# A decoder trunk in split fp32: the weights' products read their moving columns as two halves in turn

## The chip, the core and the metric

The kernel runs on one core of a Trainium2 chip. It is one program, launched once. The time is that of the device in microseconds (us); three runs of the kernel before took 2107.32 to 2107.49 us, with a median of 2107.39 us. The core's engines are TensorE (PE, with its weight loads shown apart as PEld), VectorE (DVE), ScalarE (ACT), GpSimd (POOL) and the queue engine SyncE (SP), each with its own stream of instructions; they wait for one another by semaphores. Tiles lie in SBUF, 128 partitions wide; TensorE writes into accumulators in PSUM.

## What is computed

The reference is two layers of a decoder on 256 tokens of width 2048, in float32. Cut to what matters:

```python
def reference(x, ...):                       # x: (1, 256, 2048)
    for i in range(2):
        h = rms_norm(x, attn_norm[i])
        if i == 0:   # 16 heads of 128: q, k, v = h @ wq, h @ wk, h @ wv; norm and rotary per head
            y = moba_attention(h, ...)       # causal within the one block of 256 keys, then @ wo
        else:        # low rank: (h @ wq_a) -> norm -> @ wq_b;  (h @ wkv_a) -> norm -> @ wkv_b
            y = mla_attention(h, ...)        # 16 heads of 128 plus 64 rotary dims, then @ wo
        x = x + y
        h = rms_norm(x, ffn_norm[i])
        g = conv3(h @ w_gate) + conv_b       # causal, per channel, over tokens; D_FF = 5632
        x = x + (silu(g) * (h @ w_up)) @ w_down
    return x
```

With 256 tokens nearly all arithmetic is tokens times weights. Every weight is read once (387.01 MB are read from HBM in all).

## The kernel before

**Three products for one.** Weights and tokens are float32. Each operand is split into a high part (rounded to float32r) and a low part (the rest). A product of tokens and weights is then the sum of three float32r products: high × high, high × low and low × high. The low × low product is left out. Attention's own small products use plain float32 for the first 128 tokens and the three parts for the others.

**The stream of weights.** The host lays all weights out in the order of their use, in 370 units. A unit is one DMA of up to 1 MB (128 partitions × 2048 numbers) into one of three `raw` buffers, issued on SP (`Stream.load`, L66). It holds four pieces of 128 × 512 (or 288). `Stream.split` (L92) makes the parts of each piece: ACT copies it into `whi` (L104) and DVE takes the difference into `wlo` (L105). There are five buffers of each part, each with room for 64 more numbers, so that a part can begin at a chosen address (`starts`, L156).

**By token** (`tok_major`, L227). For q, k, v and the low-rank projections the tokens are the stationary operand (128 tokens) and the weights move, 512 columns at a time. One piece is one slice of 128 of the contraction: 2 halves of the tokens × 3 parts = 6 products of 512 columns (L235), into one accumulator of 128 × 512 for each half of the tokens.

**By feature** (`feat_major`, L251). For the output projections, gate, up, down and `wq_a` the weights are stationary (128 × 128) and the 256 tokens move. A piece is four slices of the contraction: 4 × 3 = 12 products of 256 columns (L261, L262, L263), into an accumulator of 128 × 256. The moving operands are tiles of tokens' parts: `h` (the normed input, 16 slices), `a` (the gated activation, 44 slices), `oT` (attention's output, 16 slices), and `cqT` and `ckvT` (stationary operands by token). In each, a slice holds 256 numbers of the high part and then 256 of the low part, that is 2 KB:

```python
self.h = t[:, H_START : H_START + KD * 2 * S].rearrange("p (k s) -> p k s", k=KD)   # L277, S = 256
nc.scalar.activation(self.h[:, j, :S], xT[:, j, :], AF.Copy, scale=g)               # L279, high
lo, xT[:, j, :], g, hi.bitcast(F32), op0=ALU.mult, op1=ALU.subtract                 # L285, low
mm(o, w_hi, src[:, kt, :S], start=first and k == 0, ...)                            # L261, its read
```

**Who reads the accumulators.** Four accumulators rotate (`ps_acc`). By token, `Heads.evac` (L361, ACT), `evac_parts` (L604, ACT and DVE), `evac_values` (L615, ACT) and `kva_evac` (L836, ACT) copy them out. By feature, `residual` (L344, DVE) adds one to the residual stream `xT`; `FTile.evac_gate` (L739) and `FTile.product` (L764), both on DVE, read gate's and up's; `cq_part` (L914) reads those of `wq_a`.

**The order.** The program is a list of quanta, one for each piece of weights, in the order of the stream. Around each quantum stand the other engines' tasks: `at(q, f)` issues a task right after quantum q, `first(q, f)` right before it. The loop at the end (L1060) issues for each quantum the splits of the pieces ahead (up to four), the products of the piece, and then its tasks. Nothing is reordered later, so each engine's stream is this order.

**The stages**, with the times that the trace gives: MoBA's q, k, v and heads from 5 us, its output projection from 303, gate and up of layer 0 from 395, its down projection from 874 to about 1114, the low-rank projections and MLA's heads after that, their output projection from 1310, gate and up of layer 1 from 1386, and its down projection from 1862 to the end at 2101.

Of the kernel before, what the change touches and what calls it, by code (L numbers as in the profile page):

```python
# [52 lines left out]

class Stream:
# [37 lines left out]
    def split(self, upto):  # L92
        while self.split_to < min(upto, len(self.pieces)):
# [6 lines left out]
            lo = self.part_pool.tile([P, 512 + ROOM], F32R, name="wlo")[:, c : c + 512]  # L100
            if i == 0:
                self.nc.vector.tensor_copy(hi[:, :n], w)
            else:
                self.nc.scalar.copy(hi[:, :n], w)  # L104
            self.nc.vector.tensor_tensor(  # L105
                lo[:, :n], w, hi[:, :n].bitcast(F32), op=ALU.subtract
            )
# [8 lines left out]
def trunk(ctx: ExitStack, tc: tile.TileContext, a, out):  # L116
# [110 lines left out]
    def tok_major(state, lhs, kt, k_last, t_hi, t_lo, n):  # L227
# [5 lines left out]
        def product(t, part):  # L233
            c = (S if part == 2 else 0) + t * P
            mm(  # L235
                state["acc"][t][:, :n], src[:, kt, c : c + P], (t_lo if part == 1 else t_hi)[:, :n],
                start=kt == 0 and part == 0, stop=kt == k_last and part == 2,
            )
# [12 lines left out]
    def feat_major(state, rhs, k0, k_last, first, t_hi, t_lo, n, half=0):  # L251
# [6 lines left out]
        for k in range(n // P):  # L258
            kt = k0 + k
            w_hi, w_lo = t_hi[:, k * P : (k + 1) * P], t_lo[:, k * P : (k + 1) * P]  # L260
            mm(o, w_hi, src[:, kt, :S], start=first and k == 0, stop=False, skip_group_check=True)  # L261
            mm(o, w_hi, src[:, kt, S:], start=False, stop=False, skip_group_check=True)  # L262
            mm(o, w_lo, src[:, kt, :S], start=False, stop=kt == k_last, skip_group_check=True)  # L263


    class Norm:
# [7 lines left out]
        def high(self, j):  # L274
            if self.h is None:
                t = keep.tile([P, KD * 2 * S + 64], F32R, name="h")
                self.h = t[:, H_START : H_START + KD * 2 * S].rearrange("p (k s) -> p k s", k=KD)  # L277
            g = par[:, self.gain_col + j : self.gain_col + j + 1]
            nc.scalar.activation(self.h[:, j, :S], xT[:, j, :], AF.Copy, scale=g)  # L279

        def low(self, j):
            g = par[:, self.gain_col + j : self.gain_col + j + 1]
            hi, lo = self.h[:, j, :S], self.h[:, j, S:]
            nc.vector.scalar_tensor_tensor(
                lo, xT[:, j, :], g, hi.bitcast(F32), op0=ALU.mult, op1=ALU.subtract  # L285
# [58 lines left out]
    def residual(state, j, half):  # L344
        nc.vector.tensor_tensor(
            xT[:, j, :], xT[:, j, :], state["acc"][:, half * S : (half + 1) * S], op=ALU.add
        )
# [5 lines left out]
    class Heads:  # L353
# [7 lines left out]
        def evac(self):  # L361
# [6 lines left out]
            for t in range(NT):  # L368
                dst = self.x[:, t].rearrange("p n d -> p (n d)")
                src = self.state["acc"][t][:, : n * dh]  # L370
# [98 lines left out]
    class Head:  # L469
# [79 lines left out]
        def parted(self):  # L549
            oT = self.oT()  # L550
            hi, lo = oT[:, self.h, :S], oT[:, self.h, S:]
            nc.scalar.copy(hi, self.o[:, :S])
            nc.vector.tensor_tensor(lo, self.o[:, :S], hi.bitcast(F32), op=ALU.subtract)
# [17 lines left out]
    def moba_tiles(g):  # L571
        if g == 0:
            env["oT"] = att_pool.tile([P, H, 2 * S], F32R, name="oT", bufs=1)
# [144 lines left out]
    def open_ffn(layer):  # L718
# [6 lines left out]
        ffn["a"] = ffn["pool"].tile([P, NF, 2 * S], F32R, name="a", bufs=1)  # L725
# [4 lines left out]
    class FTile:  # L730
# [8 lines left out]
        def evac_gate(self):  # L739
            self.g = ffn["g"][self.j % 2]  # L740
            nc.vector.tensor_tensor(  # L741
                self.g[:, 2:], self.gate["acc"][:, :S], self.norm.rstd_b, op=ALU.mult
# [21 lines left out]
        def product(self):  # L764
            nc.vector.tensor_tensor(self.c, self.c, self.up["acc"][:, :S], op=ALU.mult)
# [56 lines left out]
    def open_mla():  # L822
# [4 lines left out]
        env["ckvT"] = att_pool.tile([P, 4, 2 * S], F32R, name="ckvT", bufs=1)  # L827
        env["cqT"] = att_pool.tile([P, 4, 2 * S], F32R, name="cqT", bufs=1)
# [350 lines left out]
```

## Time and profile before

| | |
|---|---|
| median of three runs | 2107.39 us |
| span of the profiled execution | 2105.5 us |
| TensorE busy | 2089.8 us, 16,732 records of products |
| weight loads busy | 2013.4 us, beside the products |
| VectorE busy | 1418.3 us |
| ScalarE busy | 1137.8 us |
| moved by DMA | 391.83 MB, 186 GB/s in the mean |
| granted TensorE clock | 1.000 |

The profiled execution's own time is its span of 2105.5 us, from its first to its last instruction; the median of the runs is 1.9 us above it. Products are pipelined: a row of 256 columns is shown with 276 ns, but the next one starts before it ends. The pace of products is read from their starts, or from a stretch's length over the number of products in it. One float32 product of the attention heads stands in the trace as up to two records.

### The profile page before, as it was taken

What the parts mean: (1) busy time and instruction counts of PE and PEld (TensorE: products, weight loads), DVE (VectorE), ACT (ScalarE), POOL (GpSimd) and SP (SyncE); (2) the same over time, 40 slices, a digit from 0 to 9 for tenths busy, and PEclk for the clock granted to TensorE, in tenths of its full rate; (3) what the DMA queues carried; (4) which work ended last, traced back from release to release, by engine and by line L of the source; (5) the groups of instructions that cost most, each with busy time, mean ns of one, the idle gap of its engine ahead of it and who ended that gap; (6) DMA issues with size and microseconds to landing.
All of it is one profiled execution on the core that took longest, in us unless ns stands there. A gap on an engine that the chain in (4) does not pass through costs nothing.

```text
span 2105.5 us, 42253 instructions
## 1 busy us (share of the span) xinstructions
PE 2089.8 (99%) x16732; PEld 2013.4 (96%) x16732; DVE 1418.3 (67%) x3084; ACT 1137.8 (54%) x2242; POOL 45.3 (2%) x37
## 2 busy tenths in 40 slices
PE   9999999999999999999999999999999999999999
PEld 7788889999999999999999789999999999999999
DVE  6777776766666766655556886777666667665554
ACT  6555555655555555555455675655555555544443
POOL 0000000000000000000000110000000000000000
PEclk9999999999999999999999999999999999999999
DMA  7445445555555555555554433555555555555553
GB/s 271 160 160 180 160 167 194 189 193 200 190 192 200 191 191 200 198 189 195 201 188 151 172 122 120 184 195 186 198 198 187 197 200 187 195 206 204 196 207 131
DMA packets 59382, 391.83 MB, mean 186 GB/s; under 512 B 6960, under 2 KB 10032, under 8 KB 13232
## 3 DMA queue, kind: packets, MB, share of 16 engines
q1 hardware_dynamic: 59040, 388.87, 52.1%
q8 instruction: 131, 2.15, 0.4%
q14 instruction: 67, 0.55, 0.1%
q10 hardware_dynamic: 144, 0.26, 0.0%
HBM read 387.01 MB, written 2.10 MB: 185 GB/s over the span
## 4 chain that ended last, share of the span: by engine, by line
PE 92%; DVE 5%; ACT 1%; issue 1%; DMA 1%; POOL 1%; SPq 0%; ACTq 0%; POOLq 0%
PE acc L263 26%; PE acc L261 26%; PE acc L262 26%; PE acc L235 11%; DVE wlo L105 1%; DVE junk L379 1%; DVE qk L405 1%; PE tp L449 1%; POOL hr L392 1%; PE tp L520 0%; ACT whi L104 0%; DMA raw<-in_moba_wq 0%; ACT qk L374 0%; PE sc L545 0%; DMA xT<-in_xT 0%
## 5 line engine op out<-in xcount | busy, mean ns | idle before, releaser
L105 DVE TENSOR_TENSOR wlo<-raw,whi 128x512 fp32r<-128x512 f32 (+1 forms) x1480 | 1000.3, 684 | 402.1 <-ACT whi L104 399.2
L104 ACT CAST whi<-raw 128x512 fp32r<-128x512 f32 (+1 forms) x1479 | 871.9, 614 | 464.0 <-PE acc L262 212.5
L261 PE MATMUL acc<-h,whi 128*128 128x256 f32 x2880 | 795.3, 276 | 0.0
L263 PE MATMUL acc<-h,wlo 128*128 128x256 f32 x2880 | 794.9, 276 | 0.0
L262 PE MATMUL acc<-h,whi 128*128 128x256 f32 x2880 | 794.9, 276 | 0.0
L262 PEld LDWEIGHTS acc<-h,whi 128*128 128x128 f32 x2880 | 540.7, 188 | 0.0
L261 PEld LDWEIGHTS acc<-h,whi 128*128 128x128 f32 x2880 | 540.6, 188 | 0.0
L263 PEld LDWEIGHTS acc<-h,wlo 128*128 128x128 f32 x2880 | 540.6, 188 | 0.0
L261 PE MATMUL acc<-a,whi 128*128 128x256 f32 x1408 | 388.6, 276 | 0.0
L262 PE MATMUL acc<-a,whi 128*128 128x256 f32 x1408 | 388.6, 276 | 0.0
L263 PE MATMUL acc<-a,wlo 128*128 128x256 f32 x1408 | 388.6, 276 | 0.0
L235 PE MATMUL acc<-whi,h 128*128 128x512 f32 (+1 forms) x896 | 277.4, 382 | 0.5 <-ACT whi L104 0.5
L261 PEld LDWEIGHTS acc<-a,whi 128*128 128x128 f32 x1408 | 264.3, 188 | 0.0
L262 PEld LDWEIGHTS acc<-a,whi 128*128 128x128 f32 x1408 | 264.3, 188 | 0.0
L263 PEld LDWEIGHTS acc<-a,wlo 128*128 128x128 f32 x1408 | 264.3, 188 | 0.0
L235 PEld LDWEIGHTS acc<-whi,h 128*128 128x128 f32 x896 | 164.7, 188 | 30.9 <-ACT whi L104 1.4
L235 PE MATMUL acc<-wlo,h 128*128 128x512 f32 (+1 forms) x448 | 170.2, 380 | 2.8 <-DVE wlo L105 2.8
L261 PE MATMUL acc<-oT,whi 128*128 128x256 f32 x512 | 143.5, 280 | 0.0
L263 PE MATMUL acc<-oT,wlo 128*128 128x256 f32 x512 | 141.7, 277 | 0.0
L262 PE MATMUL acc<-oT,whi 128*128 128x256 f32 x512 | 141.6, 277 | 0.0
L741 DVE TENSOR_TENSOR g<-acc,rstd_b 128x256 f32<-128x256 f32 x88 | 37.5, 426 | 125.7 <-PE acc L263 122.8
L748 ACT ACTIVATE c<-g,par 128x256 f32<-128x256 f32 x88 | 53.1, 603 | 108.3 <-DVE g L741 108.3
(173 smaller groups left out, 1626.7 us busy)
## 6 DMA issues: line engine op xcount, KB each, us to landing
raw<-in_ffn_gu SPq DMA_DIRECT2D x176, 1024.0 KB, 4.8
raw<-in_ffn_down SPq DMA_DIRECT2D x88, 1024.0 KB, 4.8
raw<-in_moba_wk SPq DMA_DIRECT2D x16, 1024.0 KB, 4.9
raw<-in_moba_wv SPq DMA_DIRECT2D x16, 1024.0 KB, 4.8
raw<-in_moba_wo SPq DMA_DIRECT2D x16, 1024.0 KB, 4.8
raw<-in_mla_wo SPq DMA_DIRECT2D x16, 1024.0 KB, 4.8
raw<-in_moba_wq SPq DMA_DIRECT2D x13, 1024.0 KB, 4.8
raw<-in_mla_wkv_a SPq DMA_DIRECT2D x8, 576.0 KB, 3.8
```

Of the source, the lines that this page charges most:

```text
L104: self.nc.scalar.copy(hi[:, :n], w)
L105: self.nc.vector.tensor_tensor(lo[:, :n], w, hi[:, :n].bitcast(F32), op=ALU.subtract)
L235: mm(state["acc"][t][:, :n], src[:, kt, c : c + P], (t_lo if part == 1 else t_hi)[:, :n], start=kt == 0 and part == 0, stop=kt == k_last a ...
L261: mm(o, w_hi, src[:, kt, :S], start=first and k == 0, stop=False, skip_group_check=True)
L262: mm(o, w_hi, src[:, kt, S:], start=False, stop=False, skip_group_check=True)
L263: mm(o, w_lo, src[:, kt, :S], start=False, stop=kt == k_last, skip_group_check=True)
L379: nc.vector.tensor_tensor_reduce(out=junk[:, : self.dh], in0=self.x[:, t, i], in1=self.x[:, t, i], scale=1.0, scalar=0.0, op0=ALU.mult, op ...
L392: nc.gpsimd.tensor_tensor(self.r, ms, mhalf[:, : NT * n], op=ALU.pow)
L405: nc.vector.scalar_tensor_tensor(self.x[:, t, i], self.x[:, t, i], self.r[:, c : c + 1], g, op0=ALU.mult, op1=ALU.mult,)
L449: nc.tensor.transpose(tp[:, (i * NT + t) * P : (i * NT + t + 1) * P], flat[:, t, c : c + P], ident)
L741: nc.vector.tensor_tensor(self.g[:, 2:], self.gate["acc"][:, :S], self.norm.rstd_b, op=ALU.mult)
L748: nc.scalar.activation(self.c, self.g[:, 2:], AF.Identity, bias=par[:, cb : cb + 1], scale=self.cw(2))
```

## The change

Three helpers are new. `halves` cuts a run of numbers into its first and second half; `woven` reads such a pair of halves in turn (first of the one, first of the other, second of the one, and so on); `unwoven` undoes this for a run that holds the two in turn.

The tokens' parts (`h`, `a`, `oT`, `cqT`, `ckvT`) get a new layout. A slice of 2 KB held 256 tokens' high parts and then 256 tokens' low parts; now it holds, for the first 128 tokens, their high and their low parts, and then the same for the other 128. So the two halves of one part lie 1 KB apart. A product by feature reads its 256 columns in turn from these two halves. A product by token reads its 512 columns in turn from the first and the last 256 columns of the piece of weights, again 1 KB apart; the pieces of 288 are now held in two runs of 144, 1 KB apart.

The accumulators' columns come out in turned order, since TensorE writes them one after the other as before. All who read them (those named above) now step over every second number of PSUM and write, or meet, the two halves in the usual order. The stationary operands are the same runs of 128 numbers, though by token at other addresses. The attention heads' own products are not changed. The number of instructions of each kind is the same for products, copies and transfers, and their order on each engine too.

The diff, without those hunks that do the same for further tiles (`oT`, `a`, `cqT`, `ckvT`, `kva_evac`, `kva_turn`, `cq_part`):

```diff
--- before.py
+++ after.py
@@ -49,6 +49,18 @@
 BY_TOKEN, BY_FEATURE = (8, 8), (24, 56)
 
 H_START = 8
+
+
+def halves(o):
+    return o.rearrange("p (t s) -> p t s", t=2)
+
+
+def woven(o):
+    return o.rearrange("p t s -> p s t")
+
+
+def unwoven(o):
+    return o.rearrange("p (s t) -> p t s", t=2)
 
 
 class Stream:
@@ -98,13 +110,15 @@
             b, c = self.starts(u, j)
             hi = self.part_pool.tile([P, 512 + ROOM], F32R, name="whi")[:, b : b + 512]
             lo = self.part_pool.tile([P, 512 + ROOM], F32R, name="wlo")[:, c : c + 512]
+            o_hi, o_lo = hi, lo
+            if n < 512:
+                o_hi, o_lo = (halves(o)[:, :, : n // 2] for o in (hi, lo))
+                w = halves(w)
             if i == 0:
-                self.nc.vector.tensor_copy(hi[:, :n], w)
+                self.nc.vector.tensor_copy(o_hi, w)
             else:
-                self.nc.scalar.copy(hi[:, :n], w)
-            self.nc.vector.tensor_tensor(
-                lo[:, :n], w, hi[:, :n].bitcast(F32), op=ALU.subtract
-            )
+                self.nc.scalar.copy(o_hi, w)
+            self.nc.vector.tensor_tensor(o_lo, w, o_hi.bitcast(F32), op=ALU.subtract)
             self.parts[i] = (hi, lo, n)
             self.split_to += 1
 
@@ -231,9 +245,9 @@
         src = lhs()
 
         def product(t, part):
-            c = (S if part == 2 else 0) + t * P
+            w = halves(t_lo if part == 1 else t_hi)[:, :, : n // 2]
             mm(
-                state["acc"][t][:, :n], src[:, kt, c : c + P], (t_lo if part == 1 else t_hi)[:, :n],
+                state["acc"][t][:, :n], src[:, kt, t, int(part == 2)], woven(w),
                 start=kt == 0 and part == 0, stop=kt == k_last and part == 2,
             )
 
@@ -258,9 +272,10 @@
         for k in range(n // P):
             kt = k0 + k
             w_hi, w_lo = t_hi[:, k * P : (k + 1) * P], t_lo[:, k * P : (k + 1) * P]
-            mm(o, w_hi, src[:, kt, :S], start=first and k == 0, stop=False, skip_group_check=True)
-            mm(o, w_hi, src[:, kt, S:], start=False, stop=False, skip_group_check=True)
-            mm(o, w_lo, src[:, kt, :S], start=False, stop=kt == k_last, skip_group_check=True)
+            hi, lo = (woven(src[:, kt, :, part]) for part in range(2))
+            mm(o, w_hi, hi, start=first and k == 0, stop=False, skip_group_check=True)
+            mm(o, w_hi, lo, start=False, stop=False, skip_group_check=True)
+            mm(o, w_lo, hi, start=False, stop=kt == k_last, skip_group_check=True)
 
 
     class Norm:
@@ -274,15 +289,17 @@
         def high(self, j):
             if self.h is None:
                 t = keep.tile([P, KD * 2 * S + 64], F32R, name="h")
-                self.h = t[:, H_START : H_START + KD * 2 * S].rearrange("p (k s) -> p k s", k=KD)
+                self.h = t[:, H_START : H_START + KD * 2 * S].rearrange(
+                    "p (k t a s) -> p k t a s", k=KD, t=NT, a=2
+                )
             g = par[:, self.gain_col + j : self.gain_col + j + 1]
-            nc.scalar.activation(self.h[:, j, :S], xT[:, j, :], AF.Copy, scale=g)
+            nc.scalar.activation(self.h[:, j, :, 0], halves(xT[:, j, :]), AF.Copy, scale=g)
 
         def low(self, j):
             g = par[:, self.gain_col + j : self.gain_col + j + 1]
-            hi, lo = self.h[:, j, :S], self.h[:, j, S:]
+            hi, lo = self.h[:, j, :, 0], self.h[:, j, :, 1]
             nc.vector.scalar_tensor_tensor(
-                lo, xT[:, j, :], g, hi.bitcast(F32), op0=ALU.mult, op1=ALU.subtract
+                lo, halves(xT[:, j, :]), g, hi.bitcast(F32), op0=ALU.mult, op1=ALU.subtract
             )
 
         def scaled(self, j):
@@ -342,9 +359,8 @@
 
 
     def residual(state, j, half):
-        nc.vector.tensor_tensor(
-            xT[:, j, :], xT[:, j, :], state["acc"][:, half * S : (half + 1) * S], op=ALU.add
-        )
+        x, acc = halves(xT[:, j, :]), unwoven(state["acc"][:, half * S : (half + 1) * S])
+        nc.vector.tensor_tensor(x, x, acc, op=ALU.add)
 
     def store(j):
         nc.sync.dma_start(out[:, j, :], xT[:, j, :])
@@ -366,8 +382,8 @@
                 self.x = att_pool.tile([P, NT, n, dh], F32, name="qr", bufs=1)
             self.ss = small.tile([P, NT, n], F32, name="ss")
             for t in range(NT):
-                dst = self.x[:, t].rearrange("p n d -> p (n d)")
-                src = self.state["acc"][t][:, : n * dh]
+                dst = halves(self.x[:, t].rearrange("p n d -> p (n d)"))
+                src = unwoven(self.state["acc"][t][:, : n * dh])
                 if self.scale is None:
                     nc.scalar.copy(dst, src)
                 else:
...
@@ -603,18 +620,18 @@
 
     def evac_parts(state, key, scale):
         v0, v1 = env[key]
-        hi, lo = v0[:, 0], v0[:, 1]
-        first_, second = (state["acc"][t][:, :512] for t in range(NT))
+        hi, lo = halves(v0[:, 0]), halves(v0[:, 1])
+        first_, second = (unwoven(state["acc"][t][:, :512]) for t in range(NT))
         r = scale()
         nc.scalar.activation(hi, first_, AF.Copy, scale=r[:, 0:1])
         nc.vector.scalar_tensor_tensor(
             lo, first_, r[:, 0:1], hi.bitcast(F32), op0=ALU.mult, op1=ALU.subtract
         )
-        nc.scalar.activation(v1, second, AF.Copy, scale=r[:, 1:2])
+        nc.scalar.activation(halves(v1), second, AF.Copy, scale=r[:, 1:2])
 
     def evac_values(state, key, scale):
         for t in range(NT):
-            dst, src = env[key][:, t, :], state["acc"][t][:, :512]
+            dst, src = halves(env[key][:, t, :]), unwoven(state["acc"][t][:, :512])
             if scale is None:
                 nc.scalar.copy(dst, src)
             else:
...
@@ -739,7 +756,8 @@
         def evac_gate(self):
             self.g = ffn["g"][self.j % 2]
             nc.vector.tensor_tensor(
-                self.g[:, 2:], self.gate["acc"][:, :S], self.norm.rstd_b, op=ALU.mult
+                halves(self.g[:, 2:]), unwoven(self.gate["acc"][:, :S]), halves(self.norm.rstd_b),
+                op=ALU.mult,
             )
 
         def conv_last(self):
@@ -762,16 +780,15 @@
             nc.vector.tensor_tensor(self.c, self.c, self.norm.rstd_b, op=ALU.mult)
 
         def product(self):
-            nc.vector.tensor_tensor(self.c, self.c, self.up["acc"][:, :S], op=ALU.mult)
+            c = halves(self.c)
+            nc.vector.tensor_tensor(c, c, unwoven(self.up["acc"][:, :S]), op=ALU.mult)
 
         def high(self):
-            nc.scalar.copy(ffn["a"][:, self.j, :S], self.c)
+            nc.scalar.copy(ffn["a"][:, self.j, :, 0], halves(self.c))
 
         def low(self):
-            a_ = ffn["a"]
-            nc.vector.tensor_tensor(
-                a_[:, self.j, S:], self.c, a_[:, self.j, :S].bitcast(F32), op=ALU.subtract
-            )
+            hi, lo = ffn["a"][:, self.j, :, 0], ffn["a"][:, self.j, :, 1]
+            nc.vector.tensor_tensor(lo, halves(self.c), hi.bitcast(F32), op=ALU.subtract)
 
     def plan_gate_up(layer, norm):
         for j in range(NF):
...
```

More of the change, by code (lines that the diff above doesn't have):

```diff
@@ L550, in parted @@
             oT = self.oT()
-            hi, lo = oT[:, self.h, :S], oT[:, self.h, S:]
-            nc.scalar.copy(hi, self.o[:, :S])
-            nc.vector.tensor_tensor(lo, self.o[:, :S], hi.bitcast(F32), op=ALU.subtract)
+            hi, lo = oT[:, self.h, :, 0], oT[:, self.h, :, 1]
+            o = halves(self.o[:, :S])
+            nc.scalar.copy(hi, o)
+            nc.vector.tensor_tensor(lo, o, hi.bitcast(F32), op=ALU.subtract)
         def plan(self, q, q_values):
@@ L572, in moba_tiles @@
         if g == 0:
-            env["oT"] = att_pool.tile([P, H, 2 * S], F32R, name="oT", bufs=1)
+            env["oT"] = att_pool.tile([P, H, NT, 2, P], F32R, name="oT", bufs=1)
         env["qT", g] = (
@@ L724, in open_ffn @@
         ffn["pool"] = ffn["stack"].enter_context(tc.tile_pool(name=f"ffn{layer}", bufs=2))
-        ffn["a"] = ffn["pool"].tile([P, NF, 2 * S], F32R, name="a", bufs=1)
+        ffn["a"] = ffn["pool"].tile([P, NF, NT, 2, P], F32R, name="a", bufs=1)
         ffn["g"] = [ffn["pool"].tile([P, S + 2], F32, name=f"g{i}", bufs=1) for i in range(2)]
@@ L826, in open_mla @@
         env["ckv"] = att_pool.tile([P, NT, 2 * KVN], F32, name="ckv", bufs=1)
-        env["ckvT"] = att_pool.tile([P, 4, 2 * S], F32R, name="ckvT", bufs=1)
-        env["cqT"] = att_pool.tile([P, 4, 2 * S], F32R, name="cqT", bufs=1)
-        env["oT"] = att_pool.tile([P, H, 2 * S], F32R, name="oT", bufs=1)
+        env["ckvT"] = att_pool.tile([P, 4, NT, 2, P], F32R, name="ckvT", bufs=1)
+        env["cqT"] = att_pool.tile([P, 4, NT, 2, P], F32R, name="cqT", bufs=1)
+        env["oT"] = att_pool.tile([P, H, NT, 2, P], F32R, name="oT", bufs=1)
         env["qr0"] = att_pool.tile([P, 8, P], F32, name="qr0", bufs=1)
@@ L838, in kva_evac @@
             nc.scalar.activation(
-                env["ckv"][:, t, half * KVN : (half + 1) * KVN], state["acc"][t][:, :KVN],
+                halves(env["ckv"][:, t, half * KVN : (half + 1) * KVN]),
+                unwoven(state["acc"][t][:, :KVN]),
                 AF.Copy, scale=n3.rstd[:, t : t + 1],
@@ L888, in kva_turn @@
         g = par[:, C_GKVA + r : C_GKVA + r + 1]
-        hi, lo = env["ckvT"][:, r, :S], env["ckvT"][:, r, S:]
-        nc.scalar.activation(hi, tp[:, :S], AF.Copy, scale=g)
+        hi, lo = env["ckvT"][:, r, :, 0], env["ckvT"][:, r, :, 1]
+        src = halves(tp[:, :S])
+        nc.scalar.activation(hi, src, AF.Copy, scale=g)
         nc.vector.scalar_tensor_tensor(
-            lo, tp[:, :S], g, hi.bitcast(F32), op0=ALU.mult, op1=ALU.subtract
+            lo, src, g, hi.bitcast(F32), op0=ALU.mult, op1=ALU.subtract
         )
@@ L915, in cq_part @@
         g = par[:, C_GQA + r : C_GQA + r + 1]
-        src = state["acc"][:, :S]
-        hi, lo = env["cqT"][:, r, :S], env["cqT"][:, r, S:]
+        src = unwoven(state["acc"][:, :S])
+        hi, lo = env["cqT"][:, r, :, 0], env["cqT"][:, r, :, 1]
         nc.scalar.activation(hi, src, AF.Copy, scale=g)
@@ L921, in cq_part @@
             cq["acc"] = att_pool.tile([P, S], F32, name="cacc", bufs=1)
-            nc.scalar.activation(cq["acc"], src, AF.Square)
+            nc.scalar.activation(halves(cq["acc"]), src, AF.Square)
         else:
             sq = small.tile([P, S], F32, name="nsq", bufs=3)
-            nc.scalar.activation(sq, src, AF.Square)
+            nc.scalar.activation(halves(sq), src, AF.Square)
             nc.vector.tensor_tensor(cq["acc"], cq["acc"], sq, op=ALU.add)
```

## The prediction

> **What bounds the kernel now.** I read the page first (busy shares, the slices, the chain that ended last), then the busy time of long stages, then single rows of the timeline for the pace of one product.
>
> ```profile
> PE 2089.8 (99%) x16732; PEld 2013.4 (96%) x16732; DVE 1418.3 (67%) x3084; ACT 1137.8 (54%) x2242; POOL 45.3 (2%) x37
> ...
> PEclk9999999999999999999999999999999999999999
> ...
> PE 92%; DVE 5%; ACT 1%; issue 1%; DMA 1%; POOL 1%; SPq 0%; ACTq 0%; POOLq 0%
> ```
>
> TensorE is busy 99% of the span, at full granted clock in every slice, and 92% of the chain that ended last lies on it. DVE and ACT have a third and nearly half of the span free. So the time is the number of products times the pace of one, and little else. The pace stands in the stage rows (columns: stretch, its length, then busy time and count of each engine, clock, share of DMA, GB/s):
>
> ```profile
> 394.70:872.00 477.30, 477.30 (x4212) 477.19 (x4211) 332.81 (x620) 256.45 (x487) 1.08 (x1) 1.00 0.55 193
> 874.30:1100.00 225.70, 225.70 (x1994) 225.70 (x1993) 128.39 (x211) 114.82 (x197) 0.00 (x0) 1.00 0.55 194
> ```
>
> The first is gate and up of layer 0, the second its down projection. 477.30/4212 is 113.3 ns per product of 256 columns, 225.70/1994 is 113.2. The two stages load DVE quite differently (70% and 57%), and the pace is the same: nothing outside TensorE sets it. The products by token move 512 columns:
>
> ```profile
> 199.69 0.62 PE L235 MATMUL acc<-whi,h 128*128 128x512 f32 x2
> 200.14 0.39 PE L235 MATMUL acc<-wlo,h 128*128 128x512 f32 x1
> 200.37 0.62 PE L235 MATMUL acc<-whi,h 128*128 128x512 f32 x2
> ```
>
> From 199.69 to 200.37 are three products: 0.68/3 = 226.7 ns, exactly twice 113.3. So there is no fixed part per product; whatever is lost is lost per column. How much is lost? The fp32 products of the attention heads give a measure:
>
> ```profile
> 1219.85 0.59 PE L545 MATMUL sc<-pT,room 128*128 128x256 f32 x2
> 1220.28 0.38 PE L546 MATMUL sc<-pT,room 128*128 128x128 f32 x2
> ```
>
> Two records of 256 columns start 0.43 us before the next line's: 215 ns each. These take a column in about twice the time; if such a record passes its columns twice (my estimate, from the near doubling), one pass is 107.5 ns. Against that, 113.3 has a surplus of 5.8 ns, 5.4%, which appears where a new 4-byte column is wanted at the full rate and not where it is wanted at half the rate. [...]
>
> **The change, part by part.**
>
> *Order of instructions.* Each engine issues the same work in the same order before and after; no product, copy or transfer is added or taken away. Beside them TensorE gets a few more waits on its own products, all at least 25 products back (25 × 113.3 ns = 2.8 us), so long done. I cost them at nothing; a wait that is already met still takes its place in the queue, but TensorE's queue runs ahead of the array by the weight load, whose busy share of 96% already lies under the products.
>
> *The moving read.* This is the change. These are the products it touches, L261 standing for L262 and L263, which have the same counts:
>
> ```profile
> L261 PE MATMUL acc<-h,whi 128*128 128x256 f32 x2880 | 795.3, 276 | 0.0
> L261 PE MATMUL acc<-a,whi 128*128 128x256 f32 x1408 | 388.6, 276 | 0.0
> L235 PE MATMUL acc<-whi,h 128*128 128x512 f32 x768 | 251.3, 396 | 0.5 <-ACT whi L104 0.5
> L235 PE MATMUL acc<-wlo,h 128*128 128x512 f32 x384 | 150.9, 393 | 1.1 <-DVE wlo L105 1.1
> L261 PE MATMUL acc<-oT,whi 128*128 128x256 f32 x512 | 143.5, 280 | 0.0
> L235 PE MATMUL acc<-whi,ckvT 128*128 128x512 f32 x128 | 44.9, 403 | 0.0
> L235 PE MATMUL acc<-whi,cqT 128*128 128x512 f32 x96 | 33.4, 400 | 0.0
> L235 PE MATMUL acc<-whi,h 128*128 128x288 f32 x128 | 26.1, 295 | 0.0
> L235 PE MATMUL acc<-wlo,ckvT 128*128 128x512 f32 x64 | 25.2, 394 | 0.9 <-DVE wlo L105 0.9
> L235 PE MATMUL acc<-wlo,h 128*128 128x288 f32 x64 | 19.4, 302 | 1.6 <-DVE wlo L105 1.6
> L235 PE MATMUL acc<-wlo,cqT 128*128 128x512 f32 x48 | 19.0, 395 | 2.6 <-DVE wlo L105 2.6
> ```
>
> That is 3 × (2880 + 1408 + 512) = 14,400 products of 256 columns, 768 + 384 + 128 + 96 + 64 + 48 = 1,488 of 512, and 192 of 288. At today's pace they are 1,632 + 337 + 24 us, 95% of the span. (The rows' means of 276 and 396 ns overlap one another, so the pace must be taken from starts.)
>
> No row of this trace shows a moving operand read out of order, so the new pace has to be bounded. Below: 107.5 ns, the fp32 pass. Above: 215 ns, if a column that lies 1 KB from the one before costs what a column costs in an fp32 record. I take the lower end, 107.5, for this reason: the surplus is exactly proportional to the columns, comes at the full rate and not at the half rate, and with two halves in turn each run of adjacent columns is asked for one column in two, which is the half rate. If the surplus is the price of going on to the next piece of a run, that step can now lie beside reads of the other run. Sum: 14,400 × 5.8 ns = 83.5 us; 1,488 × 11.7 ns = 17.4 us; 192 products of 288 columns give 1 us. Of the 17.4 I count 13, because by-token stages also wait for others:
>
> ```profile
> PEld acc L235 <- DVE wlo L105: 10.1, 13, 2.7
> PE acc L235 <- DVE wlo L105: 6.3, 9, 2.3
> ```
>
> [...]
>
> *Reads of the accumulators.* ACT and DVE now read them with a step of two elements. Nearest rows:
>
> ```profile
> L105 DVE TENSOR_TENSOR wlo<-raw,whi 128x512 fp32r<-128x512 f32 x1448 | 987.1, 689 | 397.1 <-ACT whi L104 394.2
> L104 ACT CAST whi<-raw 128x512 fp32r<-128x512 f32 x1447 | 859.2, 619 | 456.6 <-PE acc L262 212.5 <-DVE wlo L105 199.3 <-PE acc L235 32.1
> L741 DVE TENSOR_TENSOR g<-acc,rstd_b 128x256 f32<-128x256 f32 x88 | 37.5, 426 | 125.7 <-PE acc L263 122.8 <-ACT rstd_b L340 2.9
> L765 DVE TENSOR_TENSOR c<-c,acc 128x256 f32<-128x256 f32 x88 | 37.1, 421 | 17.6 <-PE acc L263 17.4
> L345 DVE TENSOR_TENSOR xT<-xT,acc 128x256 f32<-128x256 f32 x64 | 25.5, 420 | 67.6 <-PE acc L263 67.5
> ```
>
> 689 − 420 = 269 ns is what 256 elements cost DVE. Bounds per read: nothing, or one more 269 ns (each element at double price). In a gate and up stage that is at most 88 × 0.27 = 24 us on DVE's 333 in 477; at the new pace the stage lasts 453 us and DVE is 79% busy. It hides under the products, since four accumulators rotate. Where it does not hide is at the end of a layer, where the next products wait for the last residual (L345), and at the very end: about four places of 0.27 us. I take 1 us. The writes of parts in two runs of 128 cost ACT and DVE at most one more start per instruction; the waits of L104 and L105 (456.6 and 397.1 us idle) cover that.
>
> *What a faster TensorE asks of the others.* A megabyte of weights feeds four pieces of 12 products: 48 × 107.5 ns = 5.2 us instead of 5.4.
>
> ```profile
> raw<-in_ffn_gu SPq DMA_DIRECT2D x176, 1024.0 KB, 4.8
> ```
>
> It lands 4.8 us after its issue, with three buffers in use, and the queues are half busy (0.55 in the stage rows): no new wait. ACT's and DVE's split of a piece (619 and 689 ns) has 1.29 us instead of 1.36.
>
> Sum: −83.5 − 13 − 1 + 1 = −96.5 us, so a profiled span of 2105.5 − 96.5 = 2009. The median of the runs shown (2107.39) lies 1.9 us above the profiled span; I keep that difference: **2,011 us**.
>
> **The rivals.**
>
> *The pace belongs to this kind of product, not to the order of reading.* All rows of 256 and 512 columns at full rate have it, whichever tile they read (h, a, oT, whi), which speaks for it; that its loss is per column and missing at half rate speaks for the reading. Then only the 1 us of evacuations is left: 2,108.
>
> *Each column begins a new run (slower).* If TensorE's read holds one run of a few adjacent columns at a time, every column now leaves the run, in all 15,888 large products. It decides as soon as only one run is held. Price by the nearest row, an fp32 record: 215 − 113.3 = 101.7 ns × 14,400 = 1,464 us, and 203 × 1,488 = 302 us: about 3,875. [...]
>
> *Two runs are held, but they meet the weight load more often.* Products whose operands lie elsewhere already run slower:
>
> ```profile
> 96.08 0.28 PE L465 MATMUL sc<-pT,v 128*128 128x256 f32 x1
> 96.20 0.28 PE L466 MATMUL sc<-pT,v 128*128 128x256 f32 x1
> 96.32 0.39 PE L543 MATMUL sc<-pT,v 128*128 128x128 f32 x2
> ```
>
> 0.12 us instead of 0.113 for the same 256 columns. At that pace: 6.7 × 14,400 = 96 us and at most 13.3 × 1,488 = 20 us more: 2,200 to 2,225.
>
> **How the numbers follow.** The loss shrinks or goes: 0.60. Its own range is 1,985 (a pass of 106.5 ns, the fp32 record read with its rounding of 5 ns in favour) to 2,060 (half of the 5.8 ns stay: 2,107 − 42 − 9). The pace stays: 0.13. More meetings, 2,112 to 2,225: 0.10. One run at a time, near 3,875: 0.17. The last is the only case left out, so the range is **1,985 to 2,225**. Measurements of this kernel tell 0.2% (4 us) from no change; the cases give faster 0.60, same 0.13, slower 0.27.
>
> **What would show it.** Right: the starts of consecutive products of 256 columns 107 to 109 ns apart in the gate and up stage, 215 by token; DVE's share there near 75 to 79%; TensorE still 99% busy. The first rival: 113.3 unchanged. The second: 200 ns or more per product, with DVE and ACT half idle. The third: 118 to 121 ns, with scatter. Evacuation rows (426, 421, 420 ns) unchanged or up to 690. I am wrong about the lean if the pace of by-token products moves and that of the others does not, since both are read the same way.

## The result and the profile after

| | before | changed |
|---|---|---|
| median, us | 2107.44 (2107.32 to 2108.17, 4 runs) | 2071.81 (2070.98 to 2073.48, 4 runs) |
| profiled span, us | 2105.5 | 2071.6 |
| ratio, 95% interval | | 0.9831 (0.9817 to 0.9845) |

The changed kernel is 35.6 us faster, well beyond the 4 us that a measurement can tell. The forecast was a gain of 96 us: its direction came true, little more than a third of its size.

The page of the changed kernel (busy times, then the chain of work that ended last) is nearly that of before:

```profile
PE 2049.0 (99%) x16732; PEld 1989.3 (96%) x16732; DVE 1417.7 (68%) x3084; ACT 1133.7 (55%) x2242; POOL 45.3 (2%) x37
...
PE 92%; DVE 4%; ACT 1%; DMA 1%; issue 1%; POOL 0%; SPq 0%; ACTq 0%; DVEq 0%; POOLq 0%
```

TensorE still sets the end, with the same 16,732 records of products. So the pace of one product tells where the time went. By feature it stands in the stage rows of the changed kernel (the same stages, gate and up of layer 0 and its down projection; columns as before):

```profile
385.31:857.00 471.69, 471.69 (x4225) 471.54 (x4224) 333.91 (x622) 257.26 (x490) 1.07 (x1) 1.00 0.55 196
857.83:1080.00 222.17, 222.17 (x1992) 222.17 (x1991) 128.21 (x211) 114.17 (x196) 0.00 (x0) 1.00 0.55 196
```

471.69/4225 is 111.6 ns, 222.17/1992 is 111.5. Between the starts of consecutive products inside the stages, where no count at a border rounds the quotient, the distance is 111.67 ns, against 113.33 before. So of the 5.8 ns that the forecast took off each product, 1.67 came. By token, in the timeline of the changed kernel:

```profile
200.05 0.59 PE L249 MATMUL acc<-whi,h 128*128 128x512 f32 x2
200.48 0.38 PE L249 MATMUL acc<-wlo,h 128*128 128x512 f32 x1
200.70 0.59 PE L249 MATMUL acc<-whi,h 128*128 128x512 f32 x2
```

Three products in 0.65 us, 216 ns each (215.8 over more of them), against 226.7: here 10.9 of the 11.7 ns came. The products of 288 columns, by token too, went from some 132 to 122.5 ns. The two kinds, read in the same way, no longer run at the same pace per column: 215.8/512 is 0.421 ns, 111.67/256 is 0.436.

By stage, from the trace: gate and up of layer 0 went from 479.6 to 472.5 us, that of layer 1 from 479.6 to 472.5 as well, the down projection of layer 0 from 239.4 to 235.8, the time up to the first product with oT from 303.2 to 295.3, and the low-rank and attention part of layer 1, from its first product to the first one with oT, only from 164.4 to 163.2.

### The profile page after: what moved, and what is told of

The parts are those of the page before. It is cut to its first block, busy times and chain, and to the rows that moved or that the text cites. A ratio compares the mean times of both kernels' runs of the same rounds, so it can differ in the third digit from the quotient of the medians.

```text
span 2071.6 us, 42255 instructions
## 1 busy us (share of the span) xinstructions
PE 2049.0 (99%) x16732; PEld 1989.3 (96%) x16732; DVE 1417.7 (68%) x3084; ACT 1133.7 (55%) x2242; POOL 45.3 (2%) x37
## 4 chain that ended last, share of the span: by engine, by line
PE 92%; DVE 4%; ACT 1%; DMA 1%; issue 1%; POOL 0%; SPq 0%; ACTq 0%; DVEq 0%; POOLq 0%
PE acc L276 26%; PE acc L277 26%; PE acc L278 26%; PE acc L249 11%; DVE wlo L121 1%; DVE junk L395 1%; PE tp L465 1%; DVE qk L421 1%; PE tp L536 0%; DMA raw<-in_moba_wq 0%; ACT whi L120 0%; POOL hr L408 0%; DMA xT<-in_xT 0%; PE sc L561 0%; PE sc L502 0%
## 5 line engine op out<-in xcount | busy, mean ns | idle before, releaser
L276 PE MATMUL acc<-h,whi 128*128 128x256 f32 x2880 | 792.4, 275 | 0.0
L277 PE MATMUL acc<-h,whi 128*128 128x256 f32 x2880 | 792.0, 275 | 0.0
L278 PE MATMUL acc<-h,wlo 128*128 128x256 f32 x2880 | 792.0, 275 | 0.0
L277 PEld LDWEIGHTS acc<-h,whi 128*128 128x128 f32 x2880 | 553.0, 192 | 0.0
L278 PEld LDWEIGHTS acc<-h,wlo 128*128 128x128 f32 x2880 | 553.0, 192 | 0.0
L276 PEld LDWEIGHTS acc<-h,whi 128*128 128x128 f32 x2880 | 553.0, 192 | 0.0
L276 PE MATMUL acc<-a,whi 128*128 128x256 f32 x1408 | 387.2, 275 | 0.0
L277 PE MATMUL acc<-a,whi 128*128 128x256 f32 x1408 | 387.2, 275 | 0.0
L278 PE MATMUL acc<-a,wlo 128*128 128x256 f32 x1408 | 387.2, 275 | 0.0
L276 PEld LDWEIGHTS acc<-a,whi 128*128 128x128 f32 x1408 | 270.3, 192 | 0.0
L277 PEld LDWEIGHTS acc<-a,whi 128*128 128x128 f32 x1408 | 270.3, 192 | 0.0
L278 PEld LDWEIGHTS acc<-a,wlo 128*128 128x128 f32 x1408 | 270.3, 192 | 0.0
L249 PE MATMUL acc<-whi,h 128*128 128x512 f32 (+1 forms) x896 | 267.0, 371 | 1.4 <-ACT h L296 0.9
L276 PE MATMUL acc<-oT,whi 128*128 128x256 f32 x512 | 142.6, 278 | 0.0
L278 PE MATMUL acc<-oT,wlo 128*128 128x256 f32 x512 | 140.8, 275 | 0.0
L277 PE MATMUL acc<-oT,whi 128*128 128x256 f32 x512 | 140.8, 275 | 0.0
L758 DVE TENSOR_TENSOR g<-acc,rstd_b 128x256 f32<-128x256 f32 x88 | 37.4, 425 | 121.8 <-PE acc L278 118.9
```

Of the source, the lines that this page charges most:

```text
L249: mm(state["acc"][t][:, :n], src[:, kt, t, int(part == 2)], woven(w), start=kt == 0 and part == 0, stop=kt == k_last and part == 2,)
L276: mm(o, w_hi, hi, start=first and k == 0, stop=False, skip_group_check=True)
L277: mm(o, w_hi, lo, start=False, stop=False, skip_group_check=True)
L278: mm(o, w_lo, hi, start=False, stop=kt == k_last, skip_group_check=True)
L758: nc.vector.tensor_tensor(halves(self.g[:, 2:]), unwoven(self.gate["acc"][:, :S]), halves(self.norm.rstd_b), op=ALU.mult,)
```

## The experiments

All times are compared with 2071.81 us of the changed kernel and 2107.44 us of the kernel before (2106.98 to 2107.47 us in the experiments' own comparisons). The kernels with a range beside their time ran four times, the others once. Diffs are against the changed kernel and show its main lines. Line numbers of the wide kernel and of the three kernels that try orders stand a few lines later than those of the changed kernel.

### Each kind of product alone

The first kernel keeps the turned reading by token and reads straight by feature:

```diff
-            hi, lo = (woven(src[:, kt, :, part]) for part in range(2))
+            hi, lo = (src[:, kt, :, part] for part in range(2))
...
-    x, acc = halves(xT[:, j, :]), unwoven(state["acc"][:, half * S : (half + 1) * S])
+    x, acc = halves(xT[:, j, :]), halves(state["acc"][:, half * S : (half + 1) * S])
```

> Products by token read in turn as in the changed kernel; products by feature read their two runs of 128 one after the other (each run still 1 KB from the other). Theory (the read in turn removes the loss per column, and by feature the load of the next 128 x 128 weights then sets the pace): by token 215.7 ns per product of 512 columns, by feature back at 113.3 ns; the time is that of the changed kernel plus 14,400 x 1.6 ns = 23 us, about 2,095. Rival (the gain comes from somewhere else, such as the new places of the parts or the other waits): by feature stays near 111.7 ns and the time near 2,072.

The second keeps it by feature and reads straight by token:

```diff
-                state["acc"][t][:, :n], src[:, kt, t, int(part == 2)], woven(w),
+                state["acc"][t][:, :n], src[:, kt, t, int(part == 2)], w,
...
-                src = unwoven(self.state["acc"][t][:, : n * dh])
+                src = halves(self.state["acc"][t][:, : n * dh])
```

> Products by feature read in turn; products by token read their 512 columns straight. Theory: by feature 111.7 ns, by token 226.7 ns; time of the changed kernel plus at most 1,488 x 11 ns = 16 us, about 2,083 to 2,088, and together with the run by token alone the two gains add up to that of the whole change. Rival (the two parts act on each other): the gains don't add up by more than 5 us.

| kernel | us | ratio to before |
|---|---|---|
| turned by token only | 2097.64 (2096.62 to 2097.75) | 0.9954 (0.9938 to 0.9971) |
| turned by feature only | 2082.61 (2081.72 to 2082.78) | 0.9882 (0.9867 to 0.9897) |

The gains are 9.8 and 24.9 us against the kernel before of their own comparison, together 34.7 of the whole's 35.6: the parts add up. By feature, 14,400 × 1.67 ns = 24.0 us is all of it. By token, 1,488 × 10.9 ns = 16.2 us and 192 × 9.5 ns = 1.8 us, 18.0 us in all, came off the products, and 9.8 us reached the end. The waits of TensorE tell where the rest went. In the kernel turned by token only:

```profile
PEld acc L249 <- DVE wlo L121: 15.5, 22, 2.9
...
PE acc L249 <- DVE wlo L121: 8.1, 10, 2.5
```

Before they were 10.1 and 6.3 us: 7.2 us more is spent waiting for low parts, and 18.0 − 7.2 = 10.8, within 1 us of the gain. The whole change shows the same pair, 15.1 and 8.4 us; TensorE's idle time in it, span less busy time, went from 15.7 to 22.6 us.

### Is it the weight load?

What holds the products by feature at 111.67 ns? The candidate is the load of the next product's weights. The page counts it busy for 96% of the span before and after (which proves nothing: it does so for the kernel below as well), and each of these products brings its own 128×128 weights, while a product by token has 215.8 ns for the same load. Another kernel therefore uses only half the width of the weights in two products of three, and so leaves out the low parts' share of half the features:

```diff
             mm(o, w_hi, hi, start=first and k == 0, stop=False, skip_group_check=True)
-            mm(o, w_hi, lo, start=False, stop=False, skip_group_check=True)
-            mm(o, w_lo, hi, start=False, stop=kt == k_last, skip_group_check=True)
+            mm(o[:64], w_hi[:, :64], lo, start=False, stop=False, skip_group_check=True)
+            mm(o[:64], w_lo[:, :64], hi, start=False, stop=kt == k_last, skip_group_check=True)
```

> As the changed kernel, but by feature the two products with a low part load 64 of the 128 weight columns (so the low parts' share of the upper 64 features is left out). The moving columns and their order are the same. Theory (the pace of 111.7 ns by feature is that of loading the next product's 128 weight columns): products during which 64 columns are loaded take 109 ns, the third one, during which 128 are loaded, 111.7; a slice of three falls from 335 to 330 ns, 4,800 x 5 = 24 us, about 2,048. Rival (the surplus of 2.5 ns over 109.2 is left in the moving read): all three stay at 111.7 ns and the time near 2,072.

It took 2047.34 us, 24.5 less. Its timeline in the gate and up stage of layer 0:

```profile
700.10 0.28 PE L276 MATMUL acc<-h,whi 128*128 128x256 f32 x1
700.21 0.27 PE L277 MATMUL acc<-h,whi 128*64 128x256 f32 x1
700.32 0.27 PE L278 MATMUL acc<-h,wlo 128*64 128x256 f32 x1
700.43 0.28 PE L276 MATMUL acc<-h,whi 128*128 128x256 f32 x1
...
701.42 0.28 PE L276 MATMUL acc<-h,whi 128*128 128x256 f32 x1
```

From 700.10 to 701.42 are four slices of three products, 330 ns each, instead of 335: two products of 109.2 ns and one of 111.7. The moving columns are the same; only the load got shorter, as the groups of this kernel show (partitions × elements, count, busy us, mean ns):

```profile
L276 PEld LDWEIGHTS acc<-h,whi 128*128 128x128 f32 x2880 | 545.5, 189 | 0.0
L277 PEld LDWEIGHTS acc<-h,whi 128*64 128x64 f32 x2880 | 398.6, 138 | 0.0
```

Each product whose weights are narrow gains about 2.5 ns, and 2 × 4,800 × 2.5 = 24 us is the whole difference in time. (The records' own means, 189 and 138 ns, overlap one another like those of products and are no price.)

Which row holds the 111.7 ns is not what was expected. With the loads beside the products:

```profile
700.32 0.27 PE L278 MATMUL acc<-h,wlo 128*64 128x256 f32 x1
700.32 0.19 PEld L276 LDWEIGHTS acc<-h,whi 128*128 128x128 f32 x1
700.43 0.28 PE L276 MATMUL acc<-h,whi 128*128 128x256 f32 x1
700.43 0.14 PEld L277 LDWEIGHTS acc<-h,whi 128*64 128x64 f32 x1
```

The load of 128 columns begins with L278 and serves L276. Over the stage L278 to L276 is 109.3 ns and L276 to L277 is 111.7: the surplus stands in the row of the product whose own weights are wide, and not, as the expectation has it, in that of the product under which they are loaded. If a product's row begins while its load has some 2.5 ns to go, this is what would be seen; so far its own width would explain it as well.

Half the weights give half the rows of output too, and it might be these that cost; the wide kernel of the next section decides that. A kernel that has the narrow weights and reads straight by feature tells whether the loss of straight reading has to do with the load:

```diff
-            hi, lo = (woven(src[:, kt, :, part]) for part in range(2))
+            hi, lo = (src[:, kt, :, part] for part in range(2))
...
-            mm(o, w_hi, lo, start=False, stop=False, skip_group_check=True)
-            mm(o, w_lo, hi, start=False, stop=kt == k_last, skip_group_check=True)
+            mm(o[:64], w_hi[:, :64], lo, start=False, stop=False, skip_group_check=True)
+            mm(o[:64], w_lo[:, :64], hi, start=False, stop=kt == k_last, skip_group_check=True)
```

> As the run by token alone (by feature straight), but the two products with a low part load 64 weight columns (the low parts' share of the upper 64 features is left out). Theory (the loss of straight reading is in the moving read): 113.3 ns for all three, 2,097. Rival (it is the meeting of the moving read with the load of weights): products under a half load fall below 113.3 ns, towards 110; time below 2,080.

2097.16 us, against 2097.64 of the same kernel with whole weights: nothing. Its timeline:

```profile
799.79 0.28 PE L276 MATMUL acc<-h,whi 128*128 128x256 f32 x1
799.90 0.28 PE L277 MATMUL acc<-h,whi 128*64 128x256 f32 x1
800.02 0.28 PE L278 MATMUL acc<-h,wlo 128*64 128x256 f32 x1
...
800.47 0.28 PE L276 MATMUL acc<-h,whi 128*128 128x256 f32 x1
```

Two slices in 0.68 us, 340 ns each: 113.3 ns per product, whatever its weights. So the straight reading's loss lies in the moving read and not in a meeting with the weight load, and there are two limits, one close under the other: 113.3 ns of straight reading, and 111.7 ns that come with whole weights.

### Fewer loads: one product of 512 columns

If the load is the limit, a kernel that loads less must gain, with all the work done. In gate, up and down the high weights meet the high and the low part of the tokens in two products; here they do it in one of 512 columns, into two halves of an accumulator, which are added afterwards (one more copy on ACT and one more addition on DVE for each tile of gate and up, one more addition for each of down):

```diff
+            if state.get("wide"):
+                mm(state["acc"], w_hi, src[:, kt].rearrange("p t a s -> p a s t"),
+                   start=first and k == 0, stop=kt == k_last, skip_group_check=True)
+            else:
+                mm(o, w_hi, hi, start=first and k == 0, stop=False, skip_group_check=True)
+                mm(o, w_hi, lo, start=False, stop=False, skip_group_check=True)
             mm(o, w_lo, hi, start=False, stop=kt == k_last, skip_group_check=True)
...
+            part = ffn["pool"].tile([P, S], F32, name="part", bufs=2)
+            nc.scalar.copy(part, state["acc"][:, S:])
+            nc.vector.tensor_tensor(part, part, state["acc"][:, :S], op=ALU.add)
```

> As the changed kernel, but in gate, up and down (4,224 slices of the contraction) the two products with the high weights become one of 512 columns (high and low tokens) into two halves of an accumulator, which are added afterwards (one more ACT copy and DVE add per gate and up tile, one more DVE add per down tile). Two loads of weights per slice instead of three, the same number of columns. Theory (by feature the load of 128 x 128 weights sets the pace): 215.7 + 111.7 = 327.4 ns per slice instead of 335, 4,224 x 7.6 = 32 us, about 2,040; DVE near 86% of gate and up, still hidden. Rival (the surplus lies in the moving read, per column): 215.7 + 5 + 111.7 = 332.4 ns, about 2,061. Second rival (DVE's and ACT's added work is late): the slice is shorter, the time is not.

2041.54 us (2039.44 to 2042.89); the ratio to the kernel before is 0.969 (0.9673 to 0.9706). It beats both kernels and computes all that they do. Its timeline and its stage row for gate and up of layer 0:

```profile
800.07 0.38 PE L277 MATMUL acc<-h,whi 128*128 128x512 f32 x1
800.29 0.27 PE L282 MATMUL acc<-h,wlo 128*128 128x256 f32 x1
800.40 0.38 PE L277 MATMUL acc<-h,whi 128*128 128x512 f32 x1
800.62 0.27 PE L282 MATMUL acc<-h,wlo 128*128 128x256 f32 x1
800.73 0.38 PE L277 MATMUL acc<-h,whi 128*128 128x512 f32 x1
```

```profile
385.00:850.00 465.00, 464.95 (x2842) 427.31 (x2841) 369.69 (x714) 282.10 (x581) 1.07 (x1) 1.00 0.57 200
```

Two slices take 0.66 us; over many a slice is 327.5 ns, 218.3 for the wide product and 109.2 for the other. The other has 128×128 weights and all 128 rows of output, and still runs at 109.2: its load had the 218 ns of the wide product to lie under. So rows of output, or a product's own width, are not the cost; a load of 128 columns under a product of 109.2 ns is. One such load is left per slice, that of the wide product, and one surplus of 2.5 ns (218.3 − 215.8), in the row of the wide product. Saved per slice: 335 − 327.5 = 7.5 ns; by 2,816 + 1,408 slices 32 us, of which 30.3 arrived. The loads' share fell to 92% of this stage, and DVE's 370 us in 465 hide under the products.

### Does it have to be 1 KB?

By feature the two halves come 512 bytes apart here, because the two tokens' halves of one part lie side by side:

```diff
-                    "p (k t a s) -> p k t a s", k=KD, t=NT, a=2
+                    "p (k a t s) -> p k t a s", k=KD, t=NT, a=2
...
-        ffn["a"] = ffn["pool"].tile([P, NF, NT, 2, P], F32R, name="a", bufs=1)
+        ffn["a"] = ffn["pool"].tile([P, NF, 2, NT, P], F32R, name="a", bufs=1).rearrange("p k a t s -> p k t a s")
```

> By feature the two halves lie 512 bytes apart (a slice holds all high parts and then all low parts, as before the change); all else as in the changed kernel. Theory (any two runs in turn will do, as the sweep by token showed down to 32 bytes): 111.7 ns, about 2,072. Rival (1 KB is needed by feature): back to 113.3 ns or above, about 2,095.

2072.49 us, 111.7 ns per product: the same. But by feature the weight load covers what the reading does below 111.7 ns (halves 1 KB apart took 109.2 with narrow weights), so this says only that 512 bytes are no worse than that. The products by token, which have no such cover, must tell the rest.

### Orders of reading, by token

Three kernels give each of the twelve groups of products by token of the first layer (queries, keys and values, four times) another order of its 512 moving columns; the parts are held as they are, and the accumulator is read back in the order that undoes it. In the first kernel an entry gives the blocks that the 512 columns are cut into, the runs of a block that are read in turn, the numbers left free between two halves, and the number of the buffer with which the part begins (8 numbers are 32 bytes):

```diff
+SLOTS = (
+    (1, 2, 0, 8), (1, 1, 0, 8), (1, 1, 0, 0),
+    (2, 2, 0, 8), (4, 2, 0, 8), (1, 16, 0, 8),
+    (8, 2, 0, 8), (16, 2, 0, 8), (1, 128, 0, 8),
+    (32, 2, 0, 8), (1, 2, 8, 8), (1, 2, 16, 8),
+)
...
+def cut(o, blocks, runs):
+    return o.rearrange("p (b t s) -> p b t s", b=blocks, t=runs)
...
+                w = cut(w, blocks, runs).rearrange("p b t s -> p b s t")
```

> By feature as in the changed kernel. By token, each group of MoBA's q, k and v reads its 512 columns in another order: straight from 32 bytes past a multiple of 128 and straight from a multiple of 128; two runs in turn that lie 512, 256, 128, 64 and 32 bytes apart (within blocks of twice that); 16 runs in turn 128 bytes apart and 128 runs in turn 16 bytes apart; two halves 1 KB + 32 and 1 KB + 64 bytes apart. [...] Theory B (the two must lie in different kilobytes): 215.7 ns at 1 KB and a little more, 226.7 or worse below 1 KB. [...]

The second adds orders with several columns of one run in a row, and shorter distances; here against the first, and the third number of an entry is now the columns of one run in a row:

```diff
-    (1, 2, 0, 8), (1, 1, 0, 8), (1, 1, 0, 0),
-    (2, 2, 0, 8), (4, 2, 0, 8), (1, 16, 0, 8),
-    (8, 2, 0, 8), (16, 2, 0, 8), (1, 128, 0, 8),
-    (32, 2, 0, 8), (1, 2, 8, 8), (1, 2, 16, 8),
+    (1, 2, 1, 8), (64, 2, 1, 8), (1, 4, 1, 8),
+    (128, 2, 1, 8), (1, 2, 2, 8), (1, 8, 1, 8),
+    (1, 2, 4, 8), (1, 2, 8, 8), (1, 1, 1, 16),
+    (1, 2, 16, 8), (4, 4, 1, 8), (1, 32, 1, 8),
```

> By token, other orders of the 512 columns: two runs in turn 16 and 8 bytes apart; two halves 1 KB apart with 2, 4, 8 and 16 adjacent columns of each in turn; 4, 8 and 32 runs in turn (512, 256 and 64 bytes apart); 4 runs 128 bytes apart; straight from 64 past a multiple of 128. [...] Theory E (adjacent columns read right after one another cost): 2, 4, 8 and 16 in turn go up step by step towards 226.7.

The third adds orders with even columns ahead of odd ones, four runs closer together, and more columns of each half in a row; an entry gives the order in which the columns lie, and that in which they are read:

```diff
+PAIR = ("t s", "s t", {"t": 2})
+SPLIT2 = ("t s r", "r s t", {"t": 2, "r": 2})
+SPLIT4 = ("t s r", "r s t", {"t": 2, "r": 4})
+STEP2, STEP4 = (("s r", "r s", {"r": r}) for r in (2, 4))
+FOUR2, FOUR4 = (("b t s", "b s t", {"t": 4, "s": s}) for s in (2, 4))
```

> By token, orders that tell apart what the first two sweeps left open. [...]

Their whole times, 2115.47, 2146.8 and 2154.9 us, only add up good orders and bad ones. What counts is the middle value of the distances between starts of consecutive products in each group:

| order of the 512 columns | ns per product | kernel |
|---|---|---|
| two halves in turn, 1 KB apart (the change) | 216 | all three |
| 1 KB + 32 bytes, 1 KB + 64 bytes apart | 216, 216 | first |
| two runs in turn, 512, 256, 128, 64, 32 bytes apart | 216, each | first |
| two runs in turn, 16 bytes apart | 216 | second |
| two runs in turn, 8 bytes apart | 228 | second |
| straight, from 32 bytes past the start of the part's buffer | 227 | first |
| straight, from the start of the buffer, or 64 bytes past it | 234, 234 | first, second |
| two halves in turn, 2 columns of each in a row | 339 | second |
| the same, 4, 8, 16 columns in a row | 253, 244, 240 | second |
| the same, 32, 128 columns in a row | 236, 231 | third |
| 4 runs in turn, 512 and 128 bytes apart | 283, 273 | second |
| 4 runs in turn, 16 and 8 bytes apart | 268, 340 | third |
| 8 runs in turn, 256 bytes apart | 553 | second |
| 16, 32, 128 runs in turn, 128, 64, 16 bytes apart | 435, 434, 461 | first, second, first |
| two halves in turn, even columns ahead of odd | 227 | third |
| two halves in turn, in four passes of every fourth column | 452 | third |
| one run, even ahead of odd; one run, four passes | 452, 461 | third |

Three of these as rows. Sixteen runs in turn, from the timeline of the first kernel, 1.30/3 = 433 ns:

```profile
139.95 0.63 PE L277 MATMUL acc<-wlo,h 128*128 128x512 f32 x1
140.38 1.06 PE L277 MATMUL acc<-whi,h 128*128 128x512 f32 x2
141.25 0.63 PE L277 MATMUL acc<-wlo,h 128*128 128x512 f32 x1
```

Two runs 16 bytes apart, from that of the second, 0.65/3 = 217 ns:

```profile
39.65 0.60 PE L277 MATMUL acc<-whi,h 128*128 128x512 f32 x2
40.08 0.38 PE L277 MATMUL acc<-wlo,h 128*128 128x512 f32 x1
40.30 0.59 PE L277 MATMUL acc<-whi,h 128*128 128x512 f32 x2
```

Two halves with even columns ahead of odd, from that of the third, 0.68/3 = 227 ns:

```profile
39.46 0.61 PE L277 MATMUL acc<-whi,h 128*128 128x512 f32 x2
39.91 0.39 PE L277 MATMUL acc<-wlo,h 128*128 128x512 f32 x1
40.14 0.61 PE L277 MATMUL acc<-whi,h 128*128 128x512 f32 x2
```

What follows. A distance of a kilobyte plays no part (theory B): two runs in turn take 216 ns at every distance tried from 16 bytes to 1 KB + 64 bytes, and only at 8 bytes 228, about as the 227 of straight reading from the same start. Theory E asked for a rise towards 226.7 with more columns of a half in a row, and the pace fell, from 339 with two to 240 with sixteen and 231 with 128. The prediction's reason, that the other half hides a run's step to its next piece, is not borne out either: with four or more runs in turn each step lies beside reads of other runs as well, and all of these orders are slower than straight reading, 268 to 340 ns for four runs, 553 for eight and 434 to 461 for sixteen and more.

The third kernel shows that two distant runs in turn are not enough by themselves: with even columns ahead of odd in each half, the same two halves 1 KB apart take 227 instead of 216, and in four passes of every fourth column 452. One run with even columns ahead takes 452 too, twice the 227 of straight reading. Neither the two theories nor the prediction's reason give the rest of the table: the 553 of eight runs lies above the 435 of sixteen, four runs 8 bytes apart take 340 where the others of four take 268 to 283, and straight reading takes 234 from two of the starts and 227 from the third. How TensorE fetches its columns has no record in a trace. Why straight reading takes 227 ns where two runs in turn take 216 was not shown.

## Why the prediction was right or wrong

**What bounds the kernel** was read rightly: TensorE's pace sets the end, and DVE, ACT and the transfers don't enter, but for the waits on the low parts by token. The gains of both parts follow from the products' pace and these waits within 1 us. The result lies inside the range of 1,985 to 2,225, but in none of its cases: that of a loss that shrinks or goes ended at 2,060. That it would shrink came true; the reason given for it, a step that lies beside reads of the other run, was not borne out by the orders tried (four and more runs in turn took 268 to 553 ns, straight reading 227), so the direction was in part luck.

**The pace is no property of the product.** The first rival falls with both kernels that turn one kind only. **One run at a time** falls too: no product of the changed kernel doubled, and two runs in turn are faster than straight reading, 216 against 227 ns. Four and more runs in turn are slower than straight reading, 268 to 553 ns. **Two runs that meet the weight load more often** falls: no pace rose.

**The step that failed is the moving read's term, 14,400 × 5.8 ns = 83.5 us.** It measured 14,400 × 1.67 = 24.0 us, 59 us less, nearly the whole error of 61. Its lower bound of 107.5 ns was half of an fp32 record of 215 ns, which says nothing of what a new load of weights for every product takes: where each product of 256 columns brings a load of 128 columns, no run came below 111.7 ns. The prediction had the loads' row, busy for 96% of the span, and set them aside as lying under the products. They did, as long as those took 113.3 ns (there, narrow weights changed nothing: 2097.16 us against 2097.64). (The share could not have told: in the narrow kernel it is 96% as well, 1964.2 of 2045.5 us.) Of the missing 4.2 ns per product (111.7 − 107.5), 2.5 are the load, since products with a narrow or a covered load run at 109.2. The other 1.7 (109.2 − 107.5) belong to a fixed part of 2.5 ns, an estimate from products without this limit: those of 512 and 288 columns in the changed kernel start 215.8 and 122.5 ns apart, so a column takes 93.3/224 = 0.4166 ns, and 215.8 − 512 × 0.4166 leaves 2.5. By the same figures 256 columns take 109.2.

A fixed part the prediction had ruled out, because 226.7 was exactly twice 113.3; in straight reading it does not show. With it the sum would have ended 14,400 × 1.7 = 24 us later, near 2,036, and the load, 14,400 × 2.5 = 36 us, is what stands between that and 2,072.

**By token** the size was nearly right: 10.9 of 11.7 ns per product, 215.8 where 215 was bounded. For waits on the low parts the forecast wrote off 4.4 us, and they grew by some 7; 9.8 us arrived where 14 were forecast, 13 for the products of 512 columns and 1 for those of 288. The low-rank part, with its own products by token, gained 1.2 us in all; TensorE is idle for 10.5 of its 163.2 us, where it was for 7.6 of 164.4.

**The order of instructions, the strided reads of accumulators and the transfers** cost nothing, as forecast. The reads of L758, L784 and L363 in the changed kernel, by form:

```profile
L758 DVE TENSOR_TENSOR g<-acc,rstd_b 128x256 f32<-128x256 f32 x88 | 37.4, 425 | 121.8 <-PE acc L278 118.9 <-ACT rstd_b L357 2.9
L784 DVE TENSOR_TENSOR c<-c,acc 128x256 f32<-128x256 f32 x88 | 37.3, 423 | 10.8 <-PE acc L278 0.5
L363 DVE TENSOR_TENSOR xT<-xT,acc 128x256 f32<-128x256 f32 x64 | 25.5, 420 | 65.5 <-PE acc L278 65.5
```

425, 423 and 420 ns, against 426, 421 and 420 before: a step of two elements cost nothing in these reads, and the 1 us of the sum was not needed.

**The sign by which I would be wrong** was given as a pace that moves by token and not by feature, "since both are read the same way". This is nearly what happened, 10.9 of 11.7 ns against 1.67 of 5.8, and the cause was beside the reading.

## What to carry to other kernels

Where one stream of instructions sets the time and a second one is nearly as busy beside it, ask what the second takes by itself before the first is made faster: the gain ends at the second limit, here 1.7 ns under the first. A bound taken from another instruction holds only with that instruction's companions, here a load that had twice the time. And where loads of stationary operands are the limit, fewer and wider products pay even with an extra addition behind them: 2071.8 to 2041.5 us here.

## What the runs showed of the hardware

Between products of 256 columns read as two halves in turn, each with a load of 128 columns of weights of its own, the distance was 111.7 ns; with a load of 64 columns, or with the load under a product of 512, it was 109.2. The order in which the moving columns are read changed the pace of a product by token from 216 to 553 ns; straight reading is not the best order (227 from 32 bytes past the start of the buffer), and from the start of the buffer or 64 bytes past it straight reading is worse (234). Two runs in turn reach 216 at all distances tried from 16 bytes to 1 KB + 64 bytes (8 bytes apart, 228), and every order tried that takes two or more columns of a half in a row, 231 to 339, is slower than straight reading from the same start, 227.
